# Gates and branch projections with tokens stationary and 512 weight columns moving, in a pooling and state space layer on one core

## The chip, the core and the metric

One core of a Trainium2 chip runs the whole program. The metric is device time in microseconds (us), the median of the runs of the kernel. A profile is one further execution with its records: five engines run side by side, each in its own order. PE is the matrix engine (its weight loads, PEld, overlap its products), DVE and ACT are the vector and activation engines, POOL and SP mostly issue DMAs.

## The reference

One layer for 384 tokens (256 of a prompt, 8 streams of 16). `w_in` projects the normed tokens to a pool input, `z`, `x/B/C`, `dt` and two gates; the pooling branch A and the state space (SSD) branch B are projected, gated, added and projected again:

```python
u = rmsnorm(x, g_mix_pre);  proj = u @ w_in          # 2048 -> pool 2048 | z 4096 | xBC 6144 | dt 64 | gates 2 x 2048
gates = sigmoid(proj[..., OFF_GATE:])                 # two gates of 2048 columns
a_pool = pool_mixer(pool_in)                          # trailing means, per-group map, scale
xbc = silu(causal_conv(xbc));  y = ssd_scan(...)      # conv of 4 taps, chunked scan, D skip
a_ssd = gated_rmsnorm(y, z)
merged = gates[0] * (a_pool @ w_pool_proj) + gates[1] * (a_ssd @ w_ssd_proj)
x += rmsnorm(merged @ w_out);  x += rmsnorm(relu(rmsnorm(x) @ w_up)**2 @ w_down)
```

All values are fp32. The kernel writes a product as three products of a high part (fp32r) and the rest: h·h, h·l and l·h.

## The kernel before

Tokens lie in the free dimension as a row of 384 (three blocks of 128), channels on the partitions. A projection tile has 128 output channels: `proj` (or `proj_units`) loads the weights as units of 128 x 1024 (eight tiles of 128 x 128), splits each into `wh` (ACT, `wsplit`, L104) and `wl` (DVE, L105), and `half` issues 8 x 3 matmuls of `mm3` (L189 to L191): the weight tile is stationary, 384 token columns of `xgh`/`xgl` move. Only the out projection (`wo_units`, L1111 to L1113) and the down projection hold a block of 128 tokens stationary and move 512 weight columns.

The stages in order:
- norm, pool inputs and pooling (`pool_tile`, `pool_map`), then for each of 16 output tiles `gate_a(n)` (gate of branch A, tile `ga`), `pp` (projection of branch A) and their product `ma`, which POOL writes to `ma_scr`. This part is put in order by the scheduler of the framework; from the SSD stage on the order is that of the code (manual schedule).
- SSD: eight groups `g`. Each has ten projections: BT, CT and four x tiles with a convolution (`conv_units`), four z tiles (`z_units`). `items` holds them as units in PE's order, with calls in between: `block(old, new)` puts the scan's small matmuls on PE (Y, yi, pp, the transposes trx and, for a new group, trB and cb), and queues the DVE and ACT work behind them. A group has two halves: from the block that opens it (`block((g-1,1),(g,0))`, with trB and cb) to `block((g,0),(g,1))` in its middle, then on to the next group's opening block. Right after the middle block of groups 0 to 6 stands one tile of the gate of branch B, `gate_units(n)` (`gb`, two units, with a DVE multiply and an ACT sigmoid, `gbt`, L583 and L584).
- the other nine tiles of that gate, during which the last group ends and `branch_open` starts to read the branch's result back (`ar` from `a_scr`, a ring of AR = 7 tiles) and split it (`abh` on ACT, `abl` on DVE).
- `sp_units(n)`: 16 tiles of the SSD branch's projection, 4 units each; `merge` multiplies by the gate (`gbr`), adds `ma` (`mar`) and splits the sum into `mh`, `ml`, which the out projection holds stationary.
- out projection, then the MLP (more than the last third of the time), which the change leaves alone.

What sets the order on DVE and ACT in the SSD stage: `flow` issues a unit's matmuls, then the split of a later unit (`prep`, up to three ahead), then the unit's `post`, then `work(budget)`, which takes small tasks from a queue `todo` up to a budget of 2.6 a unit. A convolution's `post` (`conv_units`) is a multiply into `cbuf` on DVE (L559), the first tap on ACT (`cacc`, L563), three taps on DVE (L568), SiLU on ACT (`xs`, L572). Tasks of the queue are the decay of the state (`hs`, L735), the products `zs` (L761) with their squares on ACT (`ssum`, `ysq`), the masks `E` (L814), the state sums (`hs`, L877). `yis` (L682) is the first DVE row of a block and empties the bank of yi. Engines run in order, so a split that stands behind a task waits for it. Eight banks of PSUM are shared out by `banks(mm=..., ss=...)`: five for projections in the first stage, two in the SSD stage, whose small matmuls have six.

## Time and profile before

| what | us |
|---|---|
| median of 3 runs (2775.73 to 2778.87) | 2776.37 |
| the profiled execution, its time | 2777.25 |
| its span (first to last instruction) | 2775.1 |
| first `ga` product, last `pp` product | 165.9, 449.5 |
| first x projection of the SSD stage, last z projection | 450.1, 1275.6 |
| last `gb` product | 1360.6 |
| SSD branch projection `pj_sp` | 1361.1 to 1626.9 |
| out projection `wo` | 1627.4 to 1757.3 |
| granted PE clock, mean | 0.999 |

A row of the timeline gives start, duration, engine, line, operation, output<-inputs, count, and in brackets how long the engine stood idle before it and what ended that. A row of a group has after its shapes the count, busy time and mean in ns, then the idle time ahead. A matmul's duration overlaps the next one's: the pace of PE is the distance from start to start.

### The profile page before, as it was taken

Reading aid. Unit: us, or ns where it says so; the run is one execution under the profiler, and the core shown is the slowest. Engines: PE = TensorE matmul, PEld = TensorE weight load, DVE = VectorE, ACT = ScalarE, POOL = GpSimd, SP = SyncE. Lnnn points to the kernel's source line nnn. Section 1 sums busy time; section 2 is a strip of 40 time slices with the busy share of each in tenths; the row PEclk is TensorE's granted clock in tenths of the full one; section 3 lists DMA queues with packets and bytes.
Section 4 is the critical chain, followed back from the end, with each engine's and each line's share of the span. In section 5 each row is a group of like instructions: output and inputs, shape, how many; then the busy total and the mean of one; then the engine's idle time right before and its main releaser. Section 6 shows DMA issues by size and latency. Waiting matters only on the chain.

```text
span 2775.1 us, 40513 instructions
## 1 busy us (share of the span) xinstructions
PE 2763.2 (100%) x15873; PEld 2636.9 (95%) x15873; DVE 1844.4 (66%) x2464; ACT 1339.5 (48%) x2184; POOL 225.7 (8%) x342
## 2 busy tenths in 40 slices
PE   9999999999999999999999999999999999999998
PEld 9999999999999999999999998999999999999987
DVE  8774334567767767767733333648887788778878
ACT  6443223555555555564422233535555555555663
POOL 0000000000000000001000000000011111111221
PEclk9999999999999999999999999999999999999999
DMA  6444445555655655555844454454576767777787
GB/s 225 136 130 143 140 135 177 183 185 202 208 178 196 214 167 210 206 175 190 281 147 151 144 207 137 148 180 146 190 184 160 207 175 221 182 190 173 177 242 245
DMA packets 167615, 505.49 MB, mean 182 GB/s; under 512 B 20800, under 2 KB 44160, under 8 KB 162560
## 3 DMA queue, kind: packets, MB, share of 16 engines
q1 hardware_dynamic: 133152, 409.22, 43.3%
q0 software_dynamic: 34128, 93.68, 14.3%
q8 instruction: 124, 2.03, 0.3%
q14 instruction: 67, 0.55, 0.1%
q10 hardware_dynamic: 144, 0.01, 0.0%
HBM read 413.93 MB, written 88.90 MB: 181 GB/s over the span
## 4 chain that ended last, share of the span: by engine, by line
PE 95%; DVE 3%; issue 1%; DMA 1%; ACT 1%; SPq 0%; POOL 0%; DVEq 0%; ACTq 0%
PE pj_up L189 6%; PE pj_up L190 6%; PE pj_up L191 6%; PE pj_x L190 5%; PE pj_x L189 5%; PE pj_x L191 5%; PE wd L1448 5%; PE wd L1449 5%; PE wd L1447 5%; PE pj_sp L190 3%; PE pj_sp L189 3%; PE pj_z L190 3%; PE pj_z L191 3%; PE pj_z L189 3%; PE pj_sp L191 3%; PE pj_ga L190 2%
## 5 line engine op out<-in xcount | busy, mean ns | idle before, releaser
L1301 ACT ACTIVATE wh_wd<-raw 128x1024 fp32r<-128x1024 f32 x210 | 222.9, 1062 | 253.9 <-PE pj_up L190 104.7
L189 PE MATMUL pj_up<-x1h,wh_up 128*128 128x384 f32 x992 | 334.1, 337 | 0.0
L190 PE MATMUL pj_up<-x1l,wh_up 128*128 128x384 f32 x992 | 333.3, 336 | 0.0
L191 PE MATMUL pj_up<-x1h,wl_up 128*128 128x384 f32 x992 | 333.3, 336 | 0.0
L1302 DVE TENSOR_TENSOR wl_wd<-raw,wh_wd 128x1024 fp32r<-128x1024 f32 x210 | 256.6, 1222 | 97.1 <-ACT wh_wd L1301 96.1
L189 PE MATMUL pj_x<-xgh,wh_x 128*128 128x384 f32 x768 | 257.2, 335 | 0.0
L191 PE MATMUL pj_x<-xgh,wl_x 128*128 128x384 f32 x768 | 256.6, 334 | 0.0
L190 PE MATMUL pj_x<-xgl,wh_x 128*128 128x384 f32 x768 | 256.6, 334 | 0.0
L1448 PE MATMUL wd<-wl_wd,fh 128*128 128x512 f32 x588 | 229.1, 390 | 0.2 <-DVE wl_wd L1302 0.2
L1447 PE MATMUL wd<-wh_wd,fh 128*128 128x512 f32 x588 | 229.0, 389 | 0.0
L1449 PE MATMUL wd<-wh_wd,fl 128*128 128x512 f32 x588 | 228.8, 389 | 0.0
L1301 ACT ACTIVATE wh_up<-w_up 128x1024 fp32r<-128x1024 f32 x123 | 130.2, 1059 | 129.7 <-issue 66.5
L189 PEld LDWEIGHTS pj_up<-x1h,wh_up 128*128 128x128 f32 x992 | 186.5, 188 | 4.0
L190 PEld LDWEIGHTS pj_up<-x1l,wh_up 128*128 128x128 f32 x992 | 186.5, 188 | 4.0
L1302 DVE TENSOR_TENSOR wl_up<-w_up,wh_up 128x1024 fp32r<-128x1024 f32 x123 | 150.1, 1221 | 57.2 <-ACT wh_up L1301 57.2
L191 PEld LDWEIGHTS pj_up<-x1h,wl_up 128*128 128x128 f32 x992 | 186.5, 188 | 0.0
L191 PE MATMUL pj_z<-xgh,wl_z 128*128 128x384 f32 x512 | 171.1, 334 | 0.0
L189 PE MATMUL pj_z<-xgh,wh_z 128*128 128x384 f32 x512 | 171.0, 334 | 0.0
L190 PE MATMUL pj_z<-xgl,wh_z 128*128 128x384 f32 x512 | 171.0, 334 | 0.0
L191 PE MATMUL pj_sp<-abh,wl_sp 128*128 128x384 f32 x512 | 171.0, 334 | 0.0
L189 PE MATMUL pj_sp<-abh,wh_sp 128*128 128x384 f32 x512 | 171.0, 334 | 0.0
L190 PE MATMUL pj_sp<-abl,wh_sp 128*128 128x384 f32 x512 | 171.0, 334 | 0.0
(366 smaller groups left out, 6729.9 us busy)
## 6 DMA issues: line engine op xcount, KB each, us to landing
w_up<-w_up SPq DMA_DIRECT2D x126, 512.0 KB, 5.4
raw<-w_down SPq DMA_DIRECT2D x112, 512.0 KB, 6.3
w_x<-w_in SPq DMA_DIRECT2D x96, 512.0 KB, 4.0
acc_scr<-ev POOLq DMA_DIRECT2D x168, 256.0 KB, 5.8
w_z<-w_in SPq DMA_DIRECT2D x64, 512.0 KB, 4.5
w_sp<-w_ssd SPq DMA_DIRECT2D x64, 512.0 KB, 4.7
w_ga<-w_in SPq DMA_DIRECT2D x32, 512.0 KB, 3.4
w_pp<-w_pp SPq DMA_DIRECT2D x32, 512.0 KB, 3.4
```

The source lines that it names most:

```text
L189: te.matmul(out, wh, xh, start=first, stop=False)
L190: te.matmul(out, wh, xl, start=False, stop=False)
L191: return te.matmul(out, wl, xh, start=False, stop=last)
L1301: s.activation(h, w, AF.Copy)
L1302: return (h, l), lambda: v.tensor_tensor(l, w, h.bitcast(F32), ALU.subtract)
L1447: te.matmul(o, ah, wh[:, cols], start=c_first[c] == r and k2 == 0, stop=False)
L1448: te.matmul(o, ah, wl[:, cols], start=False, stop=False)
L1449: te.matmul(o, al, wh[:, cols], start=False, stop=c_last[c] == r and k2 == 1)
```

## The change

Gates of A and B and both branch projections change their form. The weights come in as `_moving` layout (units of 256 input rows by 512 output columns); the activations are stationary: `tokens` issues per unit and token block b two k tiles x three matmuls of 512 columns into one bank per token block. A gate or branch projection is then four blocks of 512 channels, three banks each, 8 units (16 for the SSD projection). The token scale `rstd` becomes a scale per partition, `rtok`, inside ACT's sigmoid. The merged sum has tokens on its partitions now, and `sp_turn` turns it back for the out projection: 12 PE transposes per block of 512 channels, 48 in all, each group of 12 after the first unit of the next block.

No gate tile is left in the SSD stage: the gate of B is made in two blocks (0 and 1) in the first stage, between the gate and the projection of A, and two blocks (2 and 3) in the tail after the last group. `dt_turn` stands after the first block of A's projection. The tail and the SSD projection have three projection banks (`banks(mm=3, ss=5)`), the ring AR has four tiles instead of seven.

The core of the diff (padding, the loads of the layouts on the host and renumbered columns left out):

```diff
+    def tokens(o, b, wh, wl, lhs, kp, n):
+        t = slice(b * P, b * P + P)
+        for k2 in range(2):
+            k = kp * 2 + k2
+            c = slice(k2 * 512, k2 * 512 + 512)
+            ah, al = lhs[k][0][:, t], lhs[k][1][:, t]
+            te.matmul(o, ah, wh[:, c], start=k == 0, stop=False)
+            te.matmul(o, ah, wl[:, c], start=False, stop=False)
+            te.matmul(o, al, wh[:, c], start=False, stop=k == 2 * n - 1)
...
+        v.tensor_copy(rtok, y)
...
-        def gate_a(n):
-            ps = proj(in_units(17 + n), xg, f"ga{n}")
-            t = pc2.tile([P, T], F32, tag="d", name=f"gat{n}")
-            v.tensor_tensor(t, ps, rstd, ALU.mult)
-            sg = pc2.tile([P, T], F32, tag="sg", name=f"gas{n}")
-            s.activation(sg, t, AF.Sigmoid)
+        def wide_proj(src, lhs, name, evict):
+            o = [mmtile(f"pj_{name}_{b}") for b in range(3)]
+            for kp in range(8):
+                h, l = wload(src[kp], f"{name}_{kp}")
+                for b in range(3):
+                    tokens(o[b], b, h, l, lhs, kp, 8)
+                    if kp == 7:
+                        evict(b, o[b])
+
+        def gate_block(i):
+            sg = [pc2.tile([P, 512], F32, tag="sg", name=f"gs{i}_{b}", bufs=4) for b in range(3)]
+
+            def evict(b, o):
+                s.activation(sg[b], o, AF.Sigmoid, scale=rtok[:, b : b + 1])
+                if i >= 4:
+                    gp.dma_start(gb_scr[i - 4][b], sg[b])
+
+            wide_proj(io["w_gate"][i], xg, f"{'gb' if i >= 4 else 'ga'}{i % 4}", evict)
             return sg
+
+        def branch_a(i, sg):
+            def evict(b, o):
+                v.tensor_tensor(sg[b], o, sg[b], ALU.mult)
+                gp.dma_start(ma_scr[i][b], sg[b])
+
+            wide_proj(io["w_pp"][i], A, f"pp{i}", evict)
 
...
-        sg = gate_a(0)
+        sg = gate_block(0)
         pool_map(3)
         srcs = dt_phase(pc)
-        for n in range(KD):
-            if n:
-                sg = gate_a(n)
-            if n == 2:
-                dt_turn(srcs)
-            ps = proj([io["w_pp"][n, 0], io["w_pp"][n, 1]], A, f"pp{n}")
-            m = pc2.tile([P, T], F32, tag="ma", name=f"ma{n}")
-            v.tensor_tensor(m, ps, sg, ALU.mult)
-            gp.dma_start(ma_scr[n], m)
+        branch_a(0, sg)
+        dt_turn(srcs)
+        for i in range(1, 4):
+            if i < 3:
+                gate_block(3 + i)
+            branch_a(i, gate_block(i))
...
-    def gate_units(n):
-        def post(ps):
-            t = small.tile([P, T], F32, tag="gbt", name=f"gbt{n}", bufs=2)
-            v.tensor_tensor(t, ps, rstd, ALU.mult)
-            s.activation(t, t, AF.Sigmoid)
-            gp.dma_start(gb_scr[n], t)
-
-        return proj_units(33 + n, f"gb{n}", post)
+    def gate_units(i):
+        o, out, t = [], [], {}
+
+        def evict(b):
+            if i == 2:
+                if not t:
+                    t["all"] = pd.tile([P, NB, 2 * P], F32, tag="hs", name="gbt2").rearrange("p b n -> p (b n)")
+                g = t["all"][:, b * 512 : b * 512 + 512]
+            else:
+                g = held["pe2"].tile([P, 512], F32, tag="gbt", name=f"gbt{i}_{b}", bufs=2)
+            s.activation(g, o[b], AF.Sigmoid, scale=rtok[:, b : b + 1])
+            gp.dma_start(gb_scr[i][b], g)
+
+        for kp in range(8):
+
+            def mm(hl, kp=kp):
+                if kp == 0:
+                    o.extend(mmtile(f"pj_gb{i}_{b}") for b in range(3))
+                for b in range(3):
+                    tokens(o[b], b, *hl, xg, kp, 8)
+                    if kp == 7:
+                        evict(b)
+
+            out.append((lambda kp=kp: wfetch(io["w_gate"][4 + i, kp], f"gb{i}_{kp}"), wturn, mm, nothing))
+        return out
 
...
-            if g < NG:
-                items += gate_units(gates.pop(0))
...
-    AR = 7
+    AR = 4
...
-    last_gates = [gate_units(n) for n in gates]
-    tail_ = [x for u in last_gates for x in u]
+    tail_ = gate_units(2) + gate_units(3)
+    at(lambda: banks(mm=3, ss=5))
     items += tail_[:2]
...
-    def sp_load(n):
-        if n < KD:
-            for nm, scr in (("mar", ma_scr), ("gbr", gb_scr)):
-                t = held[nm, n] = held["pe3"].tile([P, T], F32, tag=nm, name=f"{nm}{n}")
-                sy.dma_start(t, scr[n])
-
-    def sp_units(n):
-        ps, out = [], []
-
-        def merge():
-            ma, gb, o = held["mar", n], held["gbr", n], ps[0]
-            v.tensor_tensor(gb, o, gb, ALU.mult)
-            v.tensor_tensor(ma, ma, gb, ALU.add)
+    def sp_load(nb):
+        if nb < 4:
+            for b in range(3):
+                for nm, scr, pool in (("mar", ma_scr, "mpool"), ("gbr", gb_scr, "pe3")):
+                    t = held[nm, b] = held[pool].tile([P, 512], F32, tag=f"{nm}{b}", name=f"{nm}{nb}_{b}")
+                    sy.dma_start(t, scr[nb][b])
+
+    def sp_turn(nb):
+        for j in range(4):
+            n = nb * 4 + j
+            tr = sstile(f"trs{n}")[:, :T]
+            for b in range(3):
+                te.transpose(tr[:, b * P : b * P + P], held["mar", b][:, j * P : j * P + P], ident)
             h = held["mpool"].tile([P, T], F32R, name=f"mh{n}")
             l = held["mpool"].tile([P, T], F32R, name=f"ml{n}")
-            s.activation(h, ma, AF.Copy)
-            v.tensor_tensor(l, ma, h.bitcast(F32), ALU.subtract)
+            s.activation(h, tr, AF.Copy)
+            v.tensor_tensor(l, tr, h.bitcast(F32), ALU.subtract)
             ms_.append((h, l))
-            if n == KD - 1:
-                held["mpool"].tile([P, 120], F32, name="pad_mp")
-            sp_load(n + 2)
-
-        for q in range(4):
-
-            def mm(hl, q=q):
-                if q == 0:
-                    ps.append(mmtile(f"pj_sp{n}")[:, :T])
-                need(f"ab{q * 8 + 7}")
-                half(ps[0], q, hl, ab if len(ab) == 32 else ab + [None] * (32 - len(ab)))
-
-            out.append((lambda q=q: wfetch(io["w_ssd"][n, q], f"sp{n}_{q}"), wturn, mm, lambda q=q: merge() if q == 3 else None))
+        if nb == 3:
+            held["mpool"].tile([P, 120], F32, name="pad_mp")
+        sp_load(nb + 1)
+
+    def sp_units(nb):
+        o, out = [], []
+
+        def merge(b):
+            ma, gb = held["mar", b], held["gbr", b]
+            v.tensor_tensor(gb, o[b], gb, ALU.mult)
+            v.tensor_tensor(ma, ma, gb, ALU.add)
+
+        for kp in range(16):
+
+            def mm(hl, kp=kp):
+                if kp == 0:
+                    o.extend(mmtile(f"pj_sp{nb}_{b}") for b in range(3))
+                need(f"ab{kp * 2 + 1}")
+                for b in range(3):
+                    tokens(o[b], b, *hl, ab, kp, 16)
+                    if kp == 15:
+                        merge(b)
+
+            out.append(
+                (
+                    lambda kp=kp: wfetch(io["w_ssd"][nb, kp], f"sp{nb}_{kp}"),
+                    wturn,
+                    mm,
+                    lambda kp=kp: sp_turn(nb - 1) if nb and kp == 0 else sp_load(0) if not nb and kp == 2 else None,
+                )
+            )
         return out
 
-    at(lambda: (sp_load(0), sp_load(1)))
-    for n in range(KD):
-        items += sp_units(n)
+    for nb in range(4):
+        items += sp_units(nb)
...
+            if nb == 0 and kp == 0:
+                sp_turn(3)
...
```

Two places on DVE and one on PE show what moves. On DVE, the stretch behind the block in the middle of group 1, before the change: `wl_x_0` is the fifth weight split after that block, `gbt` the gate's multiply, `cbuf_4238` the convolution of the next group's BT.

```order
L105 TENSOR_TENSOR wl_x_0_6317<-w_x_0_6233,wh_x_0_6316 128x1024
L583 TENSOR_TENSOR gbt_6320<-pj_gb_6235,rstd 128x384
L735 TENSOR_TENSOR hs_1_5796<-hs_1_5796,decb 128x2048
L145 TENSOR_TENSOR wl_x_1_6353<-w_x_1_6290,wh_x_1_6352 128x1024
L761 TENSOR_TENSOR zs_0_5918<-zs_0_5918,xs_5507 128x384
L761 TENSOR_TENSOR zs_1_6005<-zs_1_6005,xs_5588 128x384
L814 TENSOR_TENSOR E_2_6268<-E_2_6268,cbm_5737 128x1024
L105 TENSOR_TENSOR wl_x_0_6390<-w_x_0_6325,wh_x_0_6389 128x1024
L559 TENSOR_TENSOR cbuf_4238<-pj_x_6327,rstd 128x24x16
L568 SCALAR_TENSOR_TENSOR cacc_6396<-cbuf_4238,vec,cacc_6396 128x384 x3
L105 TENSOR_TENSOR wl_x_1_6437<-w_x_1_6363,wh_x_1_6436 128x1024
L814 TENSOR_TENSOR E_3_6279<-E_3_6279,cbm_5737 128x1024
```

The same place now:

```order
L104 TENSOR_TENSOR wl_x_0_6199<-w_x_0_6115,wh_x_0_6198 128x1024
L587 TENSOR_TENSOR cbuf_4185<-pj_x_6117,rstd 128x24x16
L596 SCALAR_TENSOR_TENSOR cacc_6205<-cbuf_4185,vec,cacc_6205 128x384 x3
L780 TENSOR_TENSOR hs_1_5678<-hs_1_5678,decb 128x2048
L104 TENSOR_TENSOR wl_x_1_6247<-w_x_1_6172,wh_x_1_6246 128x1024
L806 TENSOR_TENSOR zs_0_5800<-zs_0_5800,xs_5389 128x384
L104 TENSOR_TENSOR wl_x_0_6280<-w_x_0_6219,wh_x_0_6279 128x1024
L587 TENSOR_TENSOR cbuf_4187<-pj_x_6221,rstd 128x24x16
L596 SCALAR_TENSOR_TENSOR cacc_6286<-cbuf_4187,vec,cacc_6286 128x384 x3
L657 TENSOR_TENSOR Cm_6294<-xs_6292,cst_161 128x256
L806 TENSOR_TENSOR zs_1_5887<-zs_1_5887,xs_5470 128x384
L144 TENSOR_TENSOR wl_x_1_6327<-w_x_1_6253,wh_x_1_6326 128x1024
```

The gate's multiply and two of its splits are gone. The first convolution stands where `gbt` stood; the decay and the two `zs`, which stood ahead of the convolution of BT, now stand behind it and behind that of CT; the masks `E_2` and `E_3` come later still.

Further on in the same stretch, on DVE, before (`cbuf_4238` is the convolution of x0 here, `su` the state sums):

```order
L145 TENSOR_TENSOR wl_x_1_6512<-w_x_1_6441,wh_x_1_6511 128x1024
L105 TENSOR_TENSOR wl_x_0_6554<-w_x_0_6484,wh_x_0_6553 128x1024
L559 TENSOR_TENSOR cbuf_4238<-pj_x_6486,rstd 128x24x16
L568 SCALAR_TENSOR_TENSOR cacc_6560<-cbuf_4238,vec,cacc_6560 128x384 x3
L877 TENSOR_TENSOR hs_1_5796<-hs_1_5796,su_1_0_6515 128x512
L877 TENSOR_TENSOR hs_1_5796<-hs_1_5796,su_1_1_6518 128x512
L105 TENSOR_TENSOR wl_x_1_6602<-w_x_1_6527,wh_x_1_6601 128x1024
L877 TENSOR_TENSOR hs_1_5796<-hs_1_5796,su_1_2_6521 128x512
L877 TENSOR_TENSOR hs_1_5796<-hs_1_5796,su_1_3_6524 128x512
L105 TENSOR_TENSOR wl_x_0_6635<-w_x_0_6574,wh_x_0_6634 128x1024
L559 TENSOR_TENSOR cbuf_4240<-pj_x_6576,rstd 128x24x16
```

and now:

```order
L859 TENSOR_TENSOR E_2_6150<-E_2_6150,cbm_5619 128x1024
L859 TENSOR_TENSOR E_3_6161<-E_3_6161,cbm_5619 128x1024
L104 TENSOR_TENSOR wl_x_0_6371<-w_x_0_6299,wh_x_0_6370 128x1024
L587 TENSOR_TENSOR cbuf_4185<-pj_x_6301,rstd 128x24x16
L596 SCALAR_TENSOR_TENSOR cacc_6377<-cbuf_4185,vec,cacc_6377 128x384 x3
L922 TENSOR_TENSOR hs_1_5678<-hs_1_5678,su_1_0_6332 128x512
L104 TENSOR_TENSOR wl_x_1_6418<-w_x_1_6344,wh_x_1_6417 128x1024
L922 TENSOR_TENSOR hs_1_5678<-hs_1_5678,su_1_1_6335 128x512
L922 TENSOR_TENSOR hs_1_5678<-hs_1_5678,su_1_2_6338 128x512
L922 TENSOR_TENSOR hs_1_5678<-hs_1_5678,su_1_3_6341 128x512
L104 TENSOR_TENSOR wl_x_0_6452<-w_x_0_6390,wh_x_0_6451 128x1024
L587 TENSOR_TENSOR cbuf_4187<-pj_x_6392,rstd 128x24x16
```

Both masks stand ahead of x0's split and convolution, and three state sums instead of two behind the split that follows. The order of ACT follows the same moves.

On PE, the end of an SSD projection tile and the start of the next, before:

```order
L190 MATMUL pj_sp_13487<-abl_13563,wh_sp_3_13554 128x384
L191 MATMUL pj_sp_13487<-abh_13562,wl_sp_3_13555 128x384
L189 MATMUL pj_sp_13638<-abh_13116,wh_sp_0_13592 128x384
L190 MATMUL pj_sp_13638<-abl_13117,wh_sp_0_13592 128x384
L191 MATMUL pj_sp_13638<-abh_13116,wl_sp_0_13593 128x384
```

and now the end of the first unit of a block's successor, where the block before it is turned (`mar` is the merged sum of token block 0, 1, 2, `cst` the identity):

```order
L208 MATMUL pj_sp_2_13227<-wl_sp_0_13190,abh_12527 128x512
L209 MATMUL pj_sp_2_13227<-wh_sp_0_13189,abl_12528 128x512
L1044 MATMUL trs_13250<-cst,mar_0_12871 128x128
L1044 MATMUL trs_13250<-cst,mar_1_12875 128x128
L1044 MATMUL trs_13250<-cst,mar_2_12879 128x128
L1044 MATMUL trs_13258<-cst,mar_0_12871 128x128
```

The columns go from 384 to 512, the weights from the stationary to the moving side, and twelve transposes (four shown) stand between two units.

More of the change, by code (lines that the diff above doesn't have):

```diff
@@ L28 @@
 NWARM = 9
-NG = 7
 NFILL = 7
@@ L239, in build @@
     a_scr = [dram.tile([P, T], F32, name=f"a_scr{i}") for i in range(32)]
-    ma_scr = [dram.tile([P, T], F32, name=f"ma_scr{i}") for i in range(16)]
-    gb_scr = [dram.tile([P, T], F32, name=f"gb_scr{i}") for i in range(16)]
+    ma_scr = [[dram.tile([P, 512], F32, name=f"ma_scr{i}_{b}") for b in range(3)] for i in range(4)]
+    gb_scr = [[dram.tile([P, 512], F32, name=f"gb_scr{i}_{b}") for b in range(3)] for i in range(4)]
     b_scr = [dram.tile([P, 2, P], F32, name=f"b_scr{i}") for i in range(G)]
@@ L255, in build @@
     rstd = small.tile([P, T], F32, name="rstd")
+    rtok = small.tile([P, 3], F32, name="rtok")
     cst2 = small.tile([P, C_END - C_MASK], F32, name="cst2")
@@ L356, in build @@
     pha.close()
-    small.tile([P, 88], F32, name="pad_small")
+    small.tile([P, 80], F32, name="pad_small")
     tok = small.tile([P, 11, NH], F32, name="tok")
@@ L366, in build @@
             bufs.append(b)
+        pc.tile([P, 112], F32, name="pad_phc")
         A = [None] * KD
@@ L596, in post @@
             S[g]["zs"][j] = z
-        return proj_units(49 + g * 10 + 6 + j, f"z{g}_{j}", post)
+        return proj_units(17 + g * 10 + 6 + j, f"z{g}_{j}", post)
     def hs_load(g, hf):
@@ L894, in build @@
     at = lambda f, *a: items.append(lambda: f(*a))
-    gates = list(range(16))
     for g in range(G):
-        u0 = 49 + g * 10
+        u0 = 17 + g * 10
         xu = lambda j: conv_units(u0 + 2 + j, g * 4 + j, "xs", 6, put(g, "xs", j))
@@ L986, in main_close @@
         held["mpool"] = mpool.enter_context(tc.tile_pool(name="mp", bufs=1, side="right", reuse_waits="tile"))
-        held["pe3"] = held["pe"].enter_context(tc.tile_pool(name="phe3", bufs=2, side="right", reuse_waits="tile"))
+        held["pe3"] = held["pe"].enter_context(tc.tile_pool(name="phe3", bufs=1, side="right", reuse_waits="tile"))
     at(main_close)
-    def sp_load(n):
-        if n < KD:
-            for nm, scr in (("mar", ma_scr), ("gbr", gb_scr)):
-                t = held[nm, n] = held["pe3"].tile([P, T], F32, tag=nm, name=f"{nm}{n}")
-                sy.dma_start(t, scr[n])
@@ L1105, in products @@
             o = wo["o", nb][b]
-            t = slice(b * P, b * P + P)
-            for k2 in range(2):
-                k = kp * 2 + k2
-                c = slice(k2 * 512, k2 * 512 + 512)
-                mh, ml = ms_[k][0][:, t], ms_[k][1][:, t]
-                te.matmul(o, mh, wh[:, c], start=k == 0, stop=False)
-                te.matmul(o, mh, wl[:, c], start=False, stop=False)
-                te.matmul(o, ml, wh[:, c], start=False, stop=k == KD - 1)
+            tokens(o, b, wh, wl, ms_, kp, 8)
         def mm(hl, kp):
@@ L1719 @@
     w_in = a["w_in"][0]
-    cols = [12288] + [i * P for i in range(16)] + [12352 + i * P for i in range(32)]
+    cols = [12288] + [i * P for i in range(16)]
     for g in range(G):
@@ L1745 @@
         ).reshape(4, 2, P, 1024),
-        "w_pp": _tiles(np, a["w_pool_proj"][0], range(0, DM, P)),
-        "w_ssd": _tiles(np, a["w_ssd_proj"][0], range(0, DM, P)),
+        "w_gate": _moving(np, w_in[:, 12352:]),
+        "w_pp": _moving(np, a["w_pool_proj"][0]),
+        "w_ssd": _moving(np, a["w_ssd_proj"][0]),
         "w_out": _moving(np, a["w_out"][0]),
```

## The prediction

> **What bounds the kernel now.** I read the page's busy shares and its chain first.
>
> ```profile
> PE 2763.2 (100%) x15873; PEld 2636.9 (95%) x15873; DVE 1844.4 (66%) x2464; ACT 1339.5 (48%) x2184; POOL 225.7 (8%) x342
> PE 95%; DVE 3%; issue 1%; DMA 1%; ACT 1%; SPq 0%; POOL 0%; DVEq 0%; ACTq 0%
> ```
>
> PE is the bound on average, so the price of one matmul comes next. The mean of a group counts the pipeline in; the pace is a window's length over the matmuls in it. The three windows lie in the pool projections with their gates, in the state space (SSD) branch projection and in the out projection. The columns are PE busy with its count, then the weight loads, DVE, ACT, POOL, the granted clock and DMA.
>
> ```profile
> 300.00:440.00 140.00, 140.00 (x808) 140.00 (x807) 51.02 (x51) 39.37 (x42) 4.85 (x9) 1.00 0.43 140
> 1420.00:1590.00 170.00, 170.00 (x983) 170.00 (x982) 66.98 (x71) 47.29 (x51) 0.00 (x0) 1.00 0.45 150
> 1640.00:1740.00 100.00, 100.00 (x442) 82.80 (x442) 39.10 (x40) 34.28 (x45) 1.10 (x2) 1.00 0.44 150
> ```
>
> A matmul with 384 columns takes 140/808 = 173.3 and 170/983 = 172.9 ns (173.1); one with 512 takes 100/442 = 226.2 ns. In these stages DVE and ACT are idle more than half the time. The SSD stage has to be read from its own order. The DVE timeline below runs from the end of a block inside group 1 to the block that opens group 2: twelve weight splits (wl), five convolutions (cbuf, cacc), and the group's small work.
>
> ```profile
> 646.41 0.41 DVE L682 TENSOR_TENSOR yis<-yi,tok 128x256 f32<-128x256 f32 x1
> ...
> 658.93 1.23 DVE L105 TENSOR_TENSOR wl_x<-w_x,wh_x 128x1024 fp32r<-128x1024 f32 x1 [7.74 <-ACT wh_x L104]
> 660.08 0.55 DVE L583 TENSOR_TENSOR gbt<-pj_gb,rstd 128x384 f32<-128x384 f32 x1
> 660.55 2.28 DVE L735 TENSOR_TENSOR hs<-hs,decb 128x2048 f32<-128x2048 f32 x1
> 662.75 1.22 DVE L145 TENSOR_TENSOR wl_x<-w_x,wh_x 128x1024 fp32r<-128x1024 f32 x1
> 663.88 1.02 DVE L761 TENSOR_TENSOR zs<-zs,xs 128x384 f32<-128x384 f32 x2
> 664.82 1.22 DVE L814 TENSOR_TENSOR E<-E,cbm 128x1024 f32<-128x1024 f32 x1
> ...
> 667.58 0.55 DVE L559 TENSOR_TENSOR cbuf<-pj_x,rstd 128x384 f32<-128x384 f32 x1
> 669.09 1.93 DVE L568 SCALAR_TENSOR_TENSOR cacc<-cbuf,vec,cacc 128x384 f32<-128x384 f32 x3 [0.96 <-ACT cacc L563]
> ...
> 676.06 0.55 DVE L559 TENSOR_TENSOR cbuf<-pj_x,rstd 128x384 f32<-128x384 f32 x1
> ...
> 680.18 0.42 DVE L612 TENSOR_TENSOR Cm<-xs,cst 128x256 f32<-128x256 f32 x1 [0.68 <-ACT xs L572]
> ...
> 683.41 0.55 DVE L559 TENSOR_TENSOR cbuf<-pj_x,rstd 128x384 f32<-128x384 f32 x1
> ...
> 686.76 1.28 DVE L877 TENSOR_TENSOR hs<-hs,su 128x512 f32<-128x512 f32 x2
> ...
> 691.96 0.55 DVE L559 TENSOR_TENSOR cbuf<-pj_x,rstd 128x384 f32<-128x384 f32 x1
> ...
> 699.30 0.55 DVE L559 TENSOR_TENSOR cbuf<-pj_x,rstd 128x384 f32<-128x384 f32 x1
> ...
> 702.65 0.42 DVE L682 TENSOR_TENSOR yis<-yi,tok 128x256 f32<-128x256 f32 x1
> ```
>
> From cbuf to cbuf it is 8.48, 7.35, 8.55 and 7.34 us, while two 24-matmul units take 8.31 us on PE. DVE is not full, but it plays ping-pong with ACT: cacc waits for ACT's first tap, ACT's SiLU waits for cacc, the next high half of a weight stands behind that SiLU, and DVE's low half behind the high half, as ACT's rows of the same stretch show (668.43 is the first tap).
>
> ```profile
> 664.46 0.53 ACT L764 ACTIVATE ssum<-zs 128x384 f32<-128x384 f32 x1 [2.32 <-DVE zs L761]
> 668.43 0.62 ACT L563 ACTIVATE cacc<-cbuf,vec 128x384 f32<-128x384 f32 x1
> 671.05 0.62 ACT L572 ACTIVATE xs<-cacc,vec 128x384 f32<-128x384 f32 x1 [0.59 <-DVE cacc L568]
> 671.57 1.99 ACT L104 ACTIVATE wh_x<-w_x 128x1024 fp32r<-128x1024 f32 x2
> ```
>
> PE's own rows at that block, and at the block that opens group 6, say what waits for the end of the stretch.
>
> ```profile
> 698.84 1.96 PE L630 MATMUL Y<-E,xdt 128*64 128x256 f32 x24
> 703.21 0.82 PE L670 MATMUL trx<-cst,xs 128*128 128x128 f32 x6
> 703.87 0.49 PE L675 MATMUL trB<-cst,xs 128*128 128x128 f32 x3
> 704.20 1.04 PE L678 MATMUL cb<-xs,xs 128*128 128x256 f32 x6
> ...
> 1126.57 0.55 PE L675 MATMUL trB<-cst,xs 128*128 128x128 f32 x3 [1.12 <-DVE yis L682]
> 1127.14 1.14 PE L678 MATMUL cb<-xs,xs 128*128 128x256 f32 x6
> ```
>
> The transposes trB need the bank that yis empties. At 703.87 PE came 0.8 us after yis ended (702.65 + 0.42); at 1126.57 it had waited 1.12 us. So before the change PE and this DVE and ACT chain are level within about a microsecond at both of these group boundaries. That is the place on which the forecast rests.
>
> **The change part by part.** *Wider columns.* 3840 matmuls (1536 gates, 768 pool, 1536 SSD projection) at 173.1 ns become 2880 at 226.2: 664.7 - 651.5 = -13.2 us, all of it PE time. The Trainium skill (TensorE: Matmul & The Clock Gate, "Wait — 56ns, not 53.3ns?") gives columns over 2.4 GHz plus about 2.5 ns; by that the gain would be estimated at 2.5 us. The windows show about 13 ns beside the columns at both widths, and the measurement decides.
>
> *Transposes.* 48 are added, 12 in each of four groups. Six trx stand 703.87 - 703.21 = 0.66 us apart from what follows: 48 x 0.11 = +5.3 us. Their splits on ACT and DVE replace equal ones. PE does not wait for the merged tiles, since a unit of the next block stands ahead of the turn.
>
> *Banks.* In the gate stage three of five banks are held by a block and three of three in the SSD projection. The next block wants a block's first bank 2.7 us or more after its last product (two token blocks of 6 x 226 ns run in between), and a copy of that size is short:
>
> ```profile
> L1459 ACT COPY ev<-wd 128x512 f32<-128x512 f32 x168 | 93.3, 572 | 5.7 <-DMA acc_scr<-ev 5.7
> ```
>
> Behind one split (1.0 on ACT, 1.2 on DVE) it would still end about in time. I take +1 us for 16 hand-overs, and 0 and +16 as the ends.
>
> *No gate in the SSD stage.* This takes two units, 8.31 us of PE, out of each of seven stretches like the one above, and only one multiply, two splits and a sigmoid from DVE and ACT. What filled the gate's time on them now stands between the convolutions. I add up the new order from the old durations. The first cbuf takes the place of gbt, 660.08. BT to CT: cacc 1.5 + 1.9, hs 2.2, split 1.1, zs 0.5, ssum on ACT 0.5, high half and split 1.1 + 1.1 = 9.9. CT to x0: Cm at +4.1, Cm and zs 0.9, a square on ACT 0.5, high half and split 1.1 + 1.1, both E masks 2.3, split 1.1 = 11.1. x0 to x1: 8.55 and one more hs sum, 0.6, outside ACT's wait = 9.2. x1 to x2: 7.35 as now. x2 to yis: 702.65 - 699.30 = 3.35. So yis starts at 660.08 + 9.9 + 11.1 + 9.2 + 7.35 + 3.35 = 701.0 and ends at 701.4, only 1.6 us earlier, where PE would be ready for trB at 703.87 - 8.31 = 695.6. PE waits 5.8 us; behind trB in its order stand cb and the next projections, which can't pass. After a wait trB and cb take 1.71 us (1126.57 to 1128.28) against 1.37 (703.87 to 705.24). Seven boundaries cost 7 x (5.8 + 0.34) = 43, less the 1.1 that is paid at one of them already: +42 us. From below, if ACT's waits hid everything that moved in, it is 0; from above, all that was taken out, 7 x (8.31 + 0.34) = +61.
>
> *The smaller ring.* Four tiles instead of seven hold the branch's read-back. Already with seven ACT waited for it:
>
> ```profile
> 1343.99 0.53 ACT L957 ACTIVATE abh<-ar 128x384 fp32r<-128x384 f32 x1 [2.48 <-DMA ar<-a_scr]
> ar<-a_scr SPq DMA_DIRECT2D x32, 192.0 KB, 4.6
> ```
>
> A round of four splits then needs 4.6 and about 0.5 on each of ACT and DVE, 5.7 us, against a unit of 18 x 226.2 ns, 4.07. Eight rounds fall back 1.6 x 8 = 13, of which the splits ahead hide up to two units, 8: between 0 and +13, I take +4. SP's weight loads stand behind these loads.
>
> *The clock.* A wait of more than 4 us can cost PE its clock. The window that ends the kernel shows it (PE's last matmul is in it, at 2765.7), and so do the warm-up products, 628 ns against 389 for the same 512 columns.
>
> ```profile
> 2765.00:2775.00 10.00, 1.09 (x5) 0.56 (x3) 6.46 (x13) 1.20 (x4) 0.00 (x0) 0.77 0.57 210
> L340 PE MATMUL warm_o<-warm 128*128 128x512 bf16 x9 | 4.0, 628 | 1.2 <-DVE warm L329 1.2
> L1111 PE MATMUL wo<-wh_wo,mh 128*128 128x512 f32 x192 | 74.7, 389 | 0.0
> ```
>
> 0.77 over 10 us is half clock for 4.6, so it fell some 4.5 us after the last matmul. The warm-up ran 4.0 us; half speed for as long costs 2. I take two of the seven waits: +4, bounds 0 and +14.
>
> Sum over the profiled execution: span 2775.1 - 13.2 + 5.3 + 1 + 42 + 4 + 4 = 2818.2. Its time was 2777.25, 2.15 above its span and 0.9 above the median of the three runs, 2776.37; so 2818.2 + 2.15 - 0.9, **2819.5 us**.
>
> **The rivals.** *PE stays the bound.* If yis were not late, because ACT and DVE run the moved work in waits that I counted as full, only the wider columns and transposes are left: 2776.4 - 13.2 + 5.3 + 0 to 5 = 2768.5 to 2773.5. It decides below a wait of (13.2 - 5.3)/7 = 1.1 us a boundary; that far, the change is not slower. For it speaks PE's share of 100%; against it that the margin at 703.87 was 0.8 us with the gate in, and that no work of the chain but the gate's three DVE rows goes.
>
> *The clock falls at each wait.* Seven instead of two: 2819.5 + 10 = 2829.5. The Trainium skill (TensorE: Matmul & The Clock Gate, "What's actually happening") says that the clock halves after at least one idle window of about 3.4 us, windows that run free of the kernel. By that rule, an estimate, a wait of 5.8 us holds a whole window in (5.8 - 3.4)/3.4, 7 of 10 cases. The window at the end of this trace agrees that the clock falls, 4.5 us on.
>
> *Half the chain shrinks*, for instance because the DMA of a boundary was the true end of some idle time: 7 x 3 = 21 instead of 42: 2798.5.
>
> **How the numbers follow.** Forecast 0.58; clock at each wait 0.20; PE the bound 0.12, of which a third lies over 0.2% below before (under 2770.8; 0.2% is what a measurement of this kernel can tell from no change); half the chain 0.10. Faster 0.04, same 0.08, slower 0.88. The range leaves out PE as the bound and the far ends: it goes from 2797 (half the chain) to 2840 (clock rival and the ring at its worst): 0.58 + 0.20 + part of the 0.10.
>
> **What would show it.** Right: trB rows with 4 to 6 us of idle before them by DVE yis at seven boundaries, groups 103 to 104 us apart instead of (1127.14 - 704.20)/4 = 105.7, 512-wide gate matmuls at 226 ns, four turns of 1.3 us without a wait, ACT waiting for ar. Wrong: groups about 97 us apart, trB without a wait. It also fails if the gate stage itself shows gaps at its block ends, or if the 512-wide products of the gates run slower than those of the out projection.

## The result and the profile after

The changed kernel takes 2839.77 us (median of 4 runs, 2837.89 to 2841.45) against 2776.65 for the kernel before: 1.0226 times as long, 95% interval 1.0208 to 1.0244. The forecast was 2819.5 with a range of 2797 to 2840, so direction and mechanism held. The size came out at the very end of the range, 0.2 us inside it, less than the runs differ among themselves: 63 us were lost where 43 had been reckoned.

First PE's row of the page and the row of the core with its mean granted clock. PE no longer fills its span, and the clock, 0.999 in the kernel before, has fallen.

```profile
PE 2780.2 (98%) x14961; PEld 2532.7 (89%) x14961; DVE 1827.2 (64%) x2421; ACT 1331.3 (47%) x2167; POOL 222.1 (8%) x334
core 0: 2839.7 us, clock 0.989
```

Then the stages, as windows from the first product of a stage to the first of the next. Columns as in the prediction: the window's length, PE busy, weight loads, DVE, ACT, POOL, granted clock, DMA. The kernel before, by its stages: gates and pool, SSD stage with the gates behind it, SSD branch projection, out projection.

```profile
165.90:450.10 284.20, 284.20 (x1645) 283.88 (x1644) 120.80 (x141) 90.17 (x101) 8.63 (x16) 1.00 0.42 138
450.10:1361.10 911.00, 909.82 (x6009) 893.60 (x6008) 641.28 (x903) 490.83 (x951) 53.55 (x101) 1.00 0.58 198
1361.10:1627.40 266.30, 266.30 (x1539) 266.30 (x1538) 109.85 (x121) 78.95 (x90) 3.04 (x6) 1.00 0.48 160
1627.40:1761.50 134.10, 134.05 (x597) 110.62 (x595) 56.23 (x69) 48.94 (x77) 2.36 (x5) 1.00 0.46 159
```

The changed kernel, the same four stages:

```profile
165.70:510.00 344.30, 344.30 (x1550) 287.70 (x1549) 130.29 (x137) 109.27 (x117) 9.31 (x18) 1.00 0.42 141
510.00:1411.30 901.30, 861.11 (x5529) 828.41 (x5527) 613.66 (x864) 459.12 (x909) 47.70 (x90) 0.98 0.55 187
1411.30:1689.50 278.20, 270.33 (x1188) 222.89 (x1189) 107.02 (x116) 82.23 (x97) 5.40 (x10) 0.98 0.50 167
1689.50:1825.00 135.50, 135.45 (x608) 111.75 (x607) 59.25 (x75) 50.19 (x80) 1.11 (x2) 1.00 0.43 148
```

Lengths can't be compared as they stand, since two gate blocks moved from the second stage into the first. What each should cost by the prediction's own prices (226.2 ns for 512 columns, 173.1 for 384, 0.11 us for a transpose) is:

| stage | before | after | change | by the prices | lost |
| --- | --- | --- | --- | --- | --- |
| gates and pool: 1440 wide products for 1536 | 284.2 | 344.3 | +60.1 | +59.8 | 0.3 |
| SSD stage and gates behind it: 288 wide for 768 | 911.0 | 901.3 | -9.7 | -67.8 | 58.1 |
| branch projection: 1152 wide for 1536, 36 transposes | 266.3 | 278.2 | +11.9 | -1.3 | 13.2 |
| out projection: 12 transposes | 134.1 | 135.5 | +1.4 | +1.3 | 0.1 |

So the form of the products costs what it was reckoned at, to a few tenths. Everything that went wrong lies in two places, and both show in PE's waits (total, times, longest), where the kernel before has only 1.1 us for trB:

```profile
PE trB L720 <- DVE yis L727: 33.1, 7, 4.7
PE pj_sp L207 <- ACT gbt L618: 6.1, 2, 4.1
PE pj_x L190 <- DVE wl_x L104: 4.4, 7, 0.6
PE pj_sp L207 <- ACT wh_sp L103: 3.0, 1, 3.0
```

The first is the wait that was forecast, at all seven group boundaries. The stretch that leads to one of them, on DVE, from the first convolution behind the middle block to yis:

```profile
719.36 0.55 DVE L587 TENSOR_TENSOR cbuf<-pj_x,rstd 128x384 f32<-128x384 f32 x1
...
729.29 0.55 DVE L587 TENSOR_TENSOR cbuf<-pj_x,rstd 128x384 f32<-128x384 f32 x1
...
740.39 0.55 DVE L587 TENSOR_TENSOR cbuf<-pj_x,rstd 128x384 f32<-128x384 f32 x1
...
749.54 0.55 DVE L587 TENSOR_TENSOR cbuf<-pj_x,rstd 128x384 f32<-128x384 f32 x1
...
756.89 0.55 DVE L587 TENSOR_TENSOR cbuf<-pj_x,rstd 128x384 f32<-128x384 f32 x1
...
760.23 0.42 DVE L727 TENSOR_TENSOR yis<-yi,tok 128x256 f32<-128x256 f32 x1
```

From cbuf to cbuf it is 9.93, 11.10, 9.15 and 7.35 us, and 3.34 to yis. The prediction had added up 9.9, 11.1, 9.2, 7.35 and 3.35 from durations of the kernel before. PE at the same boundary:

```profile
755.17 0.82 PE L715 MATMUL trx<-cst,xs 128*128 128x128 f32 x6
760.71 0.90 PE L720 MATMUL trB<-cst,xs 128*128 128x128 f32 x3 [4.72 <-DVE yis L727]
```

PE was done with trx at 755.99, 36.6 us after the first cbuf; the prediction had put it 35.5 behind (695.6 - 660.08). That is why 4.7 us are waited and not 5.8. The tile's own row, with the shortest, median and longest duration and the first and last start, gives the period of a group, (1286.7 - 553.5)/7 = 104.7 us:

```profile
L720 PE MATMUL trB<-cst,xs x24: 272/421/477, 553.5 to 1286.7; 128*128 128x128 f32 x24
```

### The profile page after: what moved, and what is told of

Same layout as the page of the kernel before. It is cut to its first block, busy times and chain, and to the rows that moved or that the text cites. A ratio compares the mean times of both kernels' runs of the same rounds, so it can differ in the third digit from the quotient of the medians.

```text
span 2839.7 us, 38568 instructions
## 1 busy us (share of the span) xinstructions
PE 2780.2 (98%) x14961; PEld 2532.7 (89%) x14961; DVE 1827.2 (64%) x2421; ACT 1331.3 (47%) x2167; POOL 222.1 (8%) x334
## 4 chain that ended last, share of the span: by engine, by line
PE 47%; DVE 3%; issue 2%; DMA 1%; ACT 1%; POOL 0%; SPq 0%; DVEq 0%; ACTq 0%; POOLq 0%
PE pj_up L188 6%; PE pj_up L189 6%; PE pj_up L190 6%; PE wd L1501 4%; PE wd L1502 4%; PE wd L1500 4%; PE pj_sp L208 3%; PE pj_sp L209 3%; PE pj_sp L207 3%; PE wo L209 2%; PE wo L207 2%; PE wo L208 2%; DMA ar<-a_scr 0%; DVE wl_wl L1355 0%; DVE ac L1571 0%
## 5 line engine op out<-in xcount | busy, mean ns | idle before, releaser
L104 DVE TENSOR_TENSOR wl_sp<-w_sp,wh_sp 128x1024 fp32r<-128x1024 f32 x64 | 78.0, 1225 | 143.0 <-ACT wh_sp L103 142.6
L1516 POOL DMA_DIRECT2D acc_scr<-ev x144 | 122.8, 900 | 572.1 <-ACT ev L1512 565.7
L207 PE MATMUL pj_sp<-wh_sp,abh 128*128 128x512 f32 x384 | 151.7, 395 | 9.1 <-ACT gbt L618 6.1
```

The lines of the kernel that those rows point to most:

```text
L207: te.matmul(o, ah, wh[:, c], start=k == 0, stop=False)
L1516: gp.dma_start(acc_scr[p][c], e, accum_op=ALU.add)
```

## The experiments

### The stage move alone (b_ng0)

The kernel before, in its old form, with all sixteen second gates behind the SSD stage:

```diff
-NG = 7
+NG = 0
```

> The kernel before with one number changed: all 16 gate tiles of the second branch come after the state space (SSD) stage, in their old form of 384 columns, instead of 7 of them inside it. Same work, same instructions, only their place moved. Theory of the chain (without the gate's 8.31 us on PE the DVE and ACT chain sets the group boundary): the same waits as in the changed kernel, 7 x 4.7 = 33 us before trB behind yis, some 4 us before weight splits, and 15 to 20 us of lower clock after the waits: 2776 + 52 to 57 = 2828 to 2834. Rival, the form (three banks per block, the tail's other banks, the wide products near the stage): nothing of that is in this kernel, 2776 plus or minus 3.

Measured: 2832.53 us, 1.0202 (1.0186 to 1.0217) of the kernel before. PE's waits:

```profile
PE trB L675 <- DVE yis L682: 33.1, 7, 4.7
PE pj_x L191 <- DVE wl_x L105: 4.4, 7, 0.6
```

They are the changed kernel's to the tenth, without a single wide product near the stage. The rival, the form, falls: 56 of the 63 us come from taking the gate out of the stage, and all that the new form did besides comes to 7.

### Idle products in the wait (a_fill20)

```diff
+            if h2 == 0 and g2:
+                fo = mmtile(f"fill{g2}")[:, :T]
+                for k in range(20):
+                    te.matmul(fo, xg[0][0][:, :P], xg[k % KD][0], start=True, stop=True)
             if h2 == 0:
                 BT, CT = d2["BT"], d2["CT"]
                 trB = sstile(f"trB{g2}")
```

> The changed kernel with 20 idle matmuls (384 columns, 173 ns each, 3.46 us) put on PE just ahead of trB at the 7 group boundaries; nothing reads their result. If PE waits 4.7 us there for the chain, they lie in the wait, which falls to 1.2 us. Theory of the clock (each wait costs a fall of the clock, paid after it): the waits become too short for it and the time falls by 14 to 18, to 2822 to 2826. If the waits alone were the cost and the clock only a number in the page: 2840. If PE were the bound: 2840 + 7 x 3.46 = 2864.

Measured: 2825.98 us, 13.8 less than the changed kernel, although PE does 140 products more. The changed kernel at one boundary, in windows of 3 us; the third column from the right is the granted clock:

```profile
756.00:759.00 3.00, 0.00 (x0) 0.00 (x0) 2.05 (x3) 0.96 (x3) 0.00 (x0) 1.00 0.00 0
759.00:762.00 3.00, 1.29 (x5) 1.14 (x6) 2.93 (x7) 1.23 (x4) 0.48 (x1) 0.52 0.00 0
762.00:765.00 3.00, 3.00 (x12) 2.91 (x11) 3.00 (x7) 2.53 (x5) 0.59 (x2) 0.50 0.23 86
765.00:768.00 3.00, 3.00 (x16) 3.00 (x16) 0.82 (x2) 2.99 (x11) 0.00 (x0) 0.84 0.85 251
```

PE waits, the clock halves while it waits, and stays at half for about 5 us after PE has begun again at 760.71 (12 and 16 products in 3 us, where 17 fit at 173.1 ns each). With the idle products, at the same boundary and over the whole run:

```profile
759.00:762.00 3.00, 2.98 (x19) 2.69 (x18) 3.00 (x8) 2.13 (x6) 1.07 (x2) 1.00 0.11 44
```

```profile
PE trB L725 <- DVE yis L732: 8.8, 7, 1.3
```

The wait is filled (8.8 + 7 x 3.46 = 33.0, as before), and the clock stays at 1.00. So the waits themselves cost the same. Not all of the 13.8 us is the price of the clock, though. In the profiled executions the SSD stage with the gates behind it is 11.5 us shorter, 889.9 for 901.3 us:

```profile
509.40:1399.30 889.90, 873.38 (x5669) 837.38 (x5668) 611.81 (x864) 459.00 (x909) 47.59 (x90) 1.00 0.55 190
```

That is the price of the clock, 1.6 us a boundary. Another 2 us lie at the start of the branch projection, where this run waited 6.9 us and the changed kernel 9.8.

### The last convolution behind yis (a_x2)

```diff
+        if tag == "xs" and c % 4 == 2 and c > 2:
+            return proj_units(ui, f"x{c}", lambda ps: kept.append(lambda: post(ps)))
         return proj_units(ui, f"x{c}", post)
...
+        while kept:
+            kept.pop()()
         if old:
             for y, j in zip(Y, (hf * 2, hf * 2 + 1)):
```

> The changed kernel with the convolution of the third x tile of a group (cbuf and cacc, in the DVE and ACT chain between the last weight splits and yis) put behind yis at the 7 boundaries; all of it still runs, the computation is the same. Theory of the chain: yis comes 3.4 us earlier, PE waits 1.2 to 1.5 us instead of 4.7 for trB, and the clock stays: 2840 - 7 x 3.4 - 15 = 2801, between 2797 and 2812. Rival (the boundary is set by something ahead of the chain, for instance a DMA or the exps on ACT): within 5 us of 2840.

Measured: 2839.07 us, no change, though the wait did what was expected:

```profile
PE trB L723 <- DVE yis L730: 9.0, 7, 1.4
PE pj_x L188 <- ACT wh_x L143: 8.4, 6, 1.4
...
PE pj_x L190 <- DVE wl_x L144: 3.9, 6, 0.6
PE pj_z L190 <- DVE wl_z L104: 3.2, 5, 0.6
```

(In the block, that `while` stands right behind the instruction that makes yis.) 24 us of waiting at the boundary are gone, and the mean clock is back to 0.995, but most of it came back as small waits inside the group: 8.4, 3.9 and 3.2 us for weight splits in the rows above, 3.1 us of `cb` for `xs`. PE's waits of the whole run fell by only 2.7 us. The theory as I had it, a chain that is too long in the second half of a group alone, falls here. The time is the rival's; of its two grounds no PE wait names a DMA, and the exps on ACT come up again below. DVE's own waits over one whole group of this run (769.6 to 874.7) say what takes its place; these are the largest of nine rows, and none of the nine names PE:

```profile
DVE wl_x L104 <- ACT wh_x L103: 10.3, 3, 7.7
DVE wl_z L144 <- ACT wh_z L143: 5.0, 1, 5.0
```

In this run DVE and ACT go round the whole group waiting for each other only (ACT's rows don't name PE either). Without the gate they are the bound in both halves, and work moved from one half to the other is not saved. The group's period says the same: from the first trB to the last it is (1276.2 - 552.9)/7 = 103.3 us with the idle products, where PE waits but runs at full clock. With the late convolution it is (1283.9 - 554.0)/7 = 104.3 us, longer still.

```profile
L725 PE MATMUL trB<-cst,xs x24: 272/273/330, 552.9 to 1276.2; 128*128 128x128 f32 x24
```

In the kernel before it is (1232.4 - 493.7)/7 = 105.5 us, all PE, of which the gate had 8.3:

```profile
L675 PE MATMUL trB<-cst,xs x24: 272/273/330, 493.7 to 1232.4; 128*128 128x128 f32 x24
```

So PE without the gate needs 97.2 us a group, and DVE with ACT 103.3. The theory to be tested from here on: shorten the turns of DVE and ACT anywhere in the group, and the time falls; move them, and it doesn't.

### The turns made shorter (a_dec, a_silu, b_silu)

The longest turn is a wait of DVE, once in each half of a group, while ACT works off a row of exponentials (exps, for the masks `E`) ahead of the next high half: 7.7 us behind the middle block, 6.9 us behind the opening one. The first of these kernels puts the decay of the state, DVE's 2.28 us that came later, into that wait:

```diff
             state_tasks(g2, h2)
+            decay_state(g2, h2)
             decay_tasks(g2, h2)
...
-            decay_state(g2, h2)
...
-        later(2.3, f"dec{g}_{hf}", decay)
+        later(0.0, f"dec{g}_{hf}", decay)
```

> The changed kernel with the decay of the state (hs, 2.28 us on DVE, once in each half of a group) moved ahead of the exps, so that DVE does it in the 7.7 us in which it waits for ACT's row of exps. Theory of the chain: 2.2 us less in each half; the wait for trB falls from 4.7 to 2.5 us, too short for the clock to fall: 7 x (105.3 - 100.5) = 34 less, 2806, between 2800 and 2815. Rival (the time is set by the amount of work on DVE, idle or not): within 5 us of 2840.

Measured: 2798.19 us, 41.6 less and 2 below the expected range, 1.0083 (1.0066 to 1.0099) of the kernel before; the period is (1248.2 - 554.1)/7 = 99.2 us. On DVE the decay now stands in the wait, which is 2.2 us shorter:

```profile
705.43 2.28 DVE L780 TENSOR_TENSOR hs<-hs,decb 128x2048 f32<-128x2048 f32 x1
713.25 1.23 DVE L104 TENSOR_TENSOR wl_x<-w_x,wh_x 128x1024 fp32r<-128x1024 f32 x1 [5.53 <-ACT wh_x L103]
```

```profile
PE trB L720 <- DVE yis L727: 12.3, 7, 1.8
```

```profile
L720 PE MATMUL trB<-cst,xs x24: 272/273/329, 554.1 to 1248.2; 128*128 128x128 f32 x24
```

The wait for trB fell by 3.0 us instead of 2.2, and the 4.4 us before weight splits are gone too. Nothing was taken out of the kernel, and two thirds of the loss is gone. The rival, that the amount of work on DVE sets the time, falls.

The second edit issues SiLU behind the next high half; a list `late` is run after each unit's split:

```diff
                 prep(i + 1)
+                flush()
                 x[3]()
...
-                s.activation(o, a, AF.Silu, bias=vec[:, V_CB + c : V_CB + c + 1])
...
+                    s.activation(o, a, AF.Silu, bias=vec[:, V_CB + c : V_CB + c + 1])
...
+                late.append(silu)
```

> The changed kernel with one edit in the order of ACT: the SiLU that ends a convolution is issued one weight unit later, behind the next high half (wh), so that a high half no longer stands behind SiLU and cacc. Same instructions. Theory of the chain (DVE and ACT in turns need 103.4 us a group, as the run with the idle matmuls showed, PE 97.4): about 1.6 us less for each of the five convolutions of the second half, more than the 4.7 us of wait; PE is then the bound again, a group takes 97.4 to 99 us instead of 105.3, and the clock stays up: 2840 - 7 x 7 = 2790, between 2785 and 2800. Rival, that DVE and ACT are simply full (their work, not their turns, makes 103.4): within 5 us of 2840.

Measured: 2820.92 us, 18.8 less, between what the two theories expected. The wait fell only from 4.7 to 3.6 us:

```profile
PE trB L732 <- DVE yis L739: 25.1, 7, 3.6
```

Of the second half's intervals from cbuf to cbuf two became shorter, 11.10 to 10.34 and 7.35 to 6.21 us; at the others the high half stood behind other work of ACT as well. My 1.6 us for each of five was wrong. The same edit in the kernel before:

> The same edit in the kernel before. Theory of the chain: with the gate's two units in the group PE needs 105.3 us and is the bound, so a shorter chain gives only the 1.4 us of waits: 2772 to 2776. Rival, that the edit shortens something that both kernels pay: 2776 - 50 = 2726.

Measured: 2774.91 us, 0.9997 (0.9988 to 1.0007): no difference. With the gate in the group PE is the bound, and a shorter chain is worth nothing.

### The start of the branch projection (a_ring3, a_r3gp, a_r3ab)

The waits of 6.1 and 3.0 us stand where the last gate block ends and the branch projection begins. ACT's rows there, in the changed kernel:

```profile
1417.72 0.69 ACT L618 ACTIVATE gbt<-pj_gb,rtok 128x512 f32<-128x512 f32 x1 [5.82 <-DMA gb_scr<-gbt]
...
1443.38 0.52 ACT L998 ACTIVATE abh<-ar 128x384 fp32r<-128x384 f32 x1 [6.67 <-DMA ar<-a_scr]
```

Three sigmoids have two tiles, so the third waits for the first one's store, and everything behind it on ACT waits too. And splits of the read-back stand on ACT ahead of high halves before their load has landed.

```diff
-                g = held["pe2"].tile([P, 512], F32, tag="gbt", name=f"gbt{i}_{b}", bufs=2)
+                g = held["pe2"].tile([P, 512], F32, tag="gbt", name=f"gbt{i}_{b}", bufs=3)
```

> The changed kernel with three tiles instead of two for the sigmoids of the last gate block (gbt), ahead of the SSD branch projection. ACT's third sigmoid waited 5.8 us there for the first one's store, and PE 6.1 us for its bank in two places. Theory that this ring is what the branch's start costs: 6 to 13 us less (the waits, and the lower clock behind them): 2827 to 2834. Rival, the ring of four for the read-back (ar) sets the same point: within 3 us of 2840.

Measured: 2834.23 us, 5.5 less, just past the edge of what was expected; 5.1 us of waits stayed. Then with the loads on another queue (`gp.dma_start(a, a_scr[i])` instead of `sy.dma_start`):

> The changed kernel with three tiles for the last gate block's sigmoids, as in the run before with that edit alone (2834), and with the read-back of the branch (ar) issued by POOL's queue instead of SP's, where it stands behind weight loads and the six loads of the merge. What is left of waits there is 2.4 + 1.5 + 1.2 = 5.1 us. Theory that the read-back comes late for its place in SP's queue: 2828 to 2831. Rival, that the ring of four tiles itself is too short: 2834 plus or minus 2.

Measured: 2838.29 us, 4 more than with three tiles alone, which neither theory had expected. The first split of the read-back waited 8.6 us for its load, now that it came from POOL's queue, so the start was later still:

```profile
1398.60 2.12 ACT L998 ACTIVATE abh<-ar 128x384 fp32r<-128x384 f32 x4 [8.61 <-DMA ar<-a_scr]
```

So taking the loads out of SP's queue did not help. Last, three tiles and a slower pace, SP's queue as it was:

```diff
-            later(0.7, f"ab{i}", lambda i=i: split(i))
+            later(1.3, f"ab{i}", lambda i=i: split(i))
```

> The changed kernel with three tiles for the last gate block's sigmoids (2834 alone) and the read-back's splits (abh, abl) issued two a weight unit instead of three to four, no earlier than they are needed. Theory that ACT runs ahead into loads that have not landed and so holds back the high halves (wh_sp) behind them, not that four tiles are too few: the waits of 2.4 + 1.5 + 1.2 us at the branch projection's start go, 2828 to 2831. Rival, the ring of four is too short at any pace: 2834 plus or minus 2, or more.

Measured: 2825.66 us, 14.1 less than the changed kernel, 8.6 less than with the three tiles and 2 better than expected. How the 14.1 us divide between the two edits is less sure: from the last gate product to the out projection's first, the profiled executions took 281.1 us in the changed kernel, 272.4 with three tiles and 265.9 here, 8.7 and 6.5 less. The branch projection, as a window from its first product to the out projection's:

```profile
1408.40:1673.80 265.40, 265.40 (x1190) 220.21 (x1189) 109.71 (x122) 84.42 (x103) 4.66 (x9) 1.00 0.50 175
```

265.4 us at full clock, with no wait, where the prices give 1152 x 0.2262 + 36 x 0.11 = 264.5. SP's queue and a ring of four tiles are enough. The ring was too short only because ACT had been told to run ahead of it.

### Put together (a_ds, a_dsx, b_ds)

> The changed kernel with the state's decay ahead of the exps (2798 alone), the SiLU behind the next high half, three sigmoid tiles and the slower pace of the read-back's splits. Theory of the chain: the wait for trB falls from 1.8 to about 0.4 us (the late SiLU gave 1.1 to 1.6 a boundary), 9 less; the branch projection's start gives 5 to 10: 2798 - 9 - 5 to 10 = 2779 to 2784. Rival, the gains lie in the same wait and don't add: 2793.

Measured: 2792.41 us, 1.0057 (1.0044 to 1.0069). The branch's start gave what it had to, no wait is left there. But the late SiLU, which alone had won 18.8 us, made the SSD stage slower on top of the early decay: the period of a group is (1254.9 - 553.7)/7 = 100.2 us, where the decay alone had 99.2. ACT's rows behind the first convolution of a second half show why. With the decay alone:

```profile
715.99 1.28 ACT L600 ACT_TABLE_LOAD   x1
717.86 0.62 ACT L600 ACTIVATE xs<-cacc,vec 128x384 f32<-128x384 f32 x1 [0.58 <-DVE cacc L596]
...
718.80 1.04 ACT L103 ACTIVATE wh_x<-w_x 128x1024 fp32r<-128x1024 f32 x1
```

and with both:

```profile
919.95 0.52 ACT L821 ACTIVATE ssum<-zs 128x384 f32<-128x384 f32 x1 [2.35 <-DVE zs L818]
920.48 1.28 ACT L610 ACT_TABLE_LOAD   x1
921.77 0.62 ACT L610 ACTIVATE xs<-cacc,vec 128x384 f32<-128x384 f32 x1
922.30 1.04 ACT L103 ACTIVATE wh_x<-w_x 128x1024 fp32r<-128x1024 f32 x1
```

Ahead of this SiLU stands a table load of 1.28 us. With the decay alone it lies in ACT's wait for the taps of DVE (`cacc`) and costs nothing. In the new order ACT first waits for `zs`, and load and SiLU both stand ahead of the high half, which SiLU was meant to let pass. DVE's split behind it waits 3.46 us (923.37) instead of 1.58 (719.87). In the second half the later SiLU wins that back, 1.1 us of it between x1 and x2, as it did alone; in the first half the same thing (3.47 us ahead of the split at 874.24, 1.54 at 671.73) isn't won back, and that is the longer period. The clock fell as well, at three of the seven boundaries. The rival's number, then, but not for its reason.

> The run before this one with the third x tile's convolution behind yis as well. That edit alone changed nothing (2839), since its 3.4 us came back in the first half of the group, where DVE and ACT were the bound too. Theory: with the decay in the exps' shadow the first half has room for it, the last wait for trB goes, PE is the bound in the whole group (97.4 to 98 us): 2774 to 2780, about level with the kernel before. Rival, the first half has no room still: 2783 to 2790.

Measured: 2776.26 us, 1.0000 (0.9991 to 1.0008) of the kernel before. The edit that changed nothing by itself is now worth 16 us: no wait for trB is left, and the period is (1240.3 - 554.2)/7 = 98.0 us, 0.8 above PE's 97.2.

```profile
PE pj_x L198 <- DVE wl_x L104: 1.7, 6, 0.3
```

```profile
L735 PE MATMUL trB<-cst,xs x24: 272/273/273, 554.2 to 1240.3; 128*128 128x128 f32 x24
```

The same edits of order in the kernel before:

> The kernel before with the same two edits of order (decay ahead of the exps, SiLU behind the next high half). Theory: PE is its bound with the gate's units in the group, so at most the 1.4 us of waits are to be had: 2773 to 2776, the same as before. Rival, that the edits shorten something of their own: below 2770.

Measured: 2777.63 us, 1.0005 (0.9996 to 1.0014): no difference. None of these kernels beats the kernel before. The decay and the later convolution without the late SiLU, with the branch's start mended, would be the next to try, since the late SiLU cost 1 us a group beside the early decay; it was not run.

## Why the prediction was right, and what was mis-sized

- *Wider columns, -13.2, and transposes, +5.3:* right. The stage table above leaves 0.3 us unexplained over 1440 wide products, and the branch projection without waits takes 265.4 for 264.5. The two paces, 173.1 and 226.2 ns, held. By the Trainium skill (TensorE: Matmul & The Clock Gate, "Wait — 56ns, not 53.3ns?") the gain would be an estimated 2.4 us, 2.5 ns for each of 960 products (the prediction wrote 2.5 us); the trace again does not show that.
- *Banks, +1:* right for the ten block ends in the gate stage, which cost 0.3 together. At the twelfth, where the last gate block ends, the step priced the sigmoid's own length and overlooked that three of them share two tiles; that is counted with the ring below.
- *The SSD stage, +42:* the step that carried the forecast, and right in its steps: the five intervals of the chain came out within 0.05 us, yis was late at seven boundaries, and the waits cost 33.1 + 4.4 + 0.7 - 1.1 = 37. PE reached the block 1.1 us later than reckoned. The waits of 0.6 us for a weight split were not in the sum. Some 7.5 us of what the stage lost no run settles: 58.1 less these 37, less 11.5 for the clock and 2 us of the wait for `gbt` that fall into this stage. A restart after each wait (priced at 0.34) may be in it.
- *Group period, 103 to 104:* the run with the idle products gives 103.3; the changed kernel itself has 104.7, because PE at half clock starts the next half late.
- *The clock, +4:* mis-sized, by 7.5. Two of seven waits were to cost 2 us each; all seven cost 1.6, 11.5 together. This is the rival "the clock falls at each wait", with its mechanism and near its price of 14, on top of the forecast's waits.
- *The smaller ring, +4 of 0 to 13:* mis-sized, by 10, above its upper bound of 13, and with the wrong reason. The branch's start cost 14.1. It was not four tiles against a load of 4.6 us: with four tiles at a slower pace nothing is lost. It was a ring of two for three sigmoids (5.5 by the medians) and splits issued ahead of their loads (8.6).
- *The rivals:* "PE stays the bound" and "half the chain" fell. The premise that DVE and ACT are level with PE held, but they are so over the whole group, where the prediction saw it in the second half alone. It made no difference to the forecast, and all the difference to the remedy.

With the clock at 11.5 and the branch's start at 14.1 the prediction's sum would have read 2837.1, 2.7 below the result. The upper end of the range had been drawn for just these two terms at their worst; that the result fell inside it, by 0.2 us, is luck.

## What to carry to other kernels

A PE share of 100% does not say that work taken from PE is saved: ask how much less the engines that feed it need for the same group of work, since a second bound can lie 2% below the first and be paid for at once. An order can be worth more than the work in it: filling the longest wait of the second bound with work that is there anyway gave 41.6 us, while moving work past the last wait gave nothing until that was done. Where a wait on PE is unavoidable, count the clock with it, and where a ring looks too short, see first who runs ahead into it.

## What the runs showed of the hardware

A wait costs the clock earlier than I had taken it, and its length alone does not decide. At 4.7 us the granted clock halved at seven boundaries of seven. At 3.6 us (the run with the late SiLU) it fell at all seven too, for a shorter time (0.92 over the 21 us from 751.5, at one of them). In the profiled executions with the early decay (1.8 us) and the idle products (1.3 us) it fell at none. But with the four edits put together PE waited 1.7 us at every one of the seven, and the clock fell at three. A boundary at which it fell, and the next, at which it did not:

```profile
745.00:766.00 21.00, 19.23 (x148) 17.80 (x147) 14.71 (x22) 14.21 (x35) 1.07 (x2) 0.92 0.48 167
846.00:867.00 21.00, 19.25 (x156) 17.81 (x156) 14.68 (x21) 14.25 (x36) 1.07 (x2) 1.00 0.48 167
```

With the last convolution behind yis it fell five times in the stage, each time at waits of at most 1.4 us. So these runs give no length of wait below which the clock is safe. The Trainium skill (TensorE: Matmul & The Clock Gate, "What's actually happening") asks for a whole idle window of about 3.4 us, and has the windows run free of the kernel. Read as in the prediction, that would be an estimated 4 of 10 waits at 4.7 us, hardly one at 3.6 and none at 1.7. Equal waits with and without a fall fit windows that run free; that a whole window must be idle does not fit. Whether the small products ahead of the wait (trx, pp, yi) count as little activity was not tested.
